# Value products with the probabilities as the stationary operand: blocks of 128 queries, normalised by query and transposed back

## The chip, the core and the metric

The kernel runs on one core of a Trainium2 chip. The metric is the device time of one execution in microseconds (us). A time given for a kernel is the median of several executions; a profile is one further execution, taken by the hardware profiler, and its times are of that execution alone. Engines are named as in the profile: PE is TensorE's stream of matmuls, PEld its loading of stationary operands (each matmul has one load ahead of it, which may run beside the matmul before), DVE is VectorE, ACT is ScalarE, POOL is GpSimd and SP is SyncE, which issues most DMAs.

## The reference

Two layers of a diffusion backbone work on 1024 latent tokens and 256 context tokens of width 1024, in float32. Layer 0 (even) holds two attentions: A, in which every query sees all 1280 keys, and B, in which a block of 128 queries sees the context and a band of three blocks, with a learned sink per head in the softmax's denominator. Each has 8 heads of 64 in 2 key/value groups. Layer 1 (odd) holds a Conformer convolution and a neighbourhood attention D with 8 heads on a 16 x 64 grid. What the change touches is the second half of every attention, the product with the values and the division by the denominator, and the gate behind it:

```python
def gqa_attend(q, k, v, bias=None, sink=None):
    s = jnp.einsum("bqhgd,bkhd->bhgqk", q, k, preferred_element_type=jnp.float32) * ATTN_SCALE
    if bias is not None:
        s = s + bias
    if sink is not None:
        sink_col = jnp.broadcast_to(sink.astype(jnp.float32)[None, :, :, None, None], s.shape[:-1] + (1,))
        p = jax.nn.softmax(jnp.concatenate([s, sink_col], axis=-1), axis=-1)[..., :-1]
    else:
        p = jax.nn.softmax(s, axis=-1)
    return jnp.einsum("bhgqk,bkhd->bqhgd", p.astype(v.dtype), v)
...
y_lat = jnp.concatenate([oa * jax.nn.silu(ag), ob * jax.nn.silu(bg)], axis=-1) @ w_out
```

## The kernel before

**Precision.** Every wide matmul is done in float32r, with operands split into a high and a low part (`hi` the rounded value, `lo` the rest): three products make one (`mm3`, lines 320 to 322). For the value product the parts are `ph` and `pl` of the probabilities and two halves of the value tile: `V[:, 0:64]` is the low part, `V[:, 64:128]` the high part, and `V[:, 128:192]` is ones, which give the denominator in 64 equal rows.

**Groups and tiles of attention.** A group is 512 columns of queries for one key/value head: 4 heads x 128 queries in layer 0, 512 queries of one head in layer 1. A tile is one block of 128 keys against these columns. Layer 0 has 40 groups (`group0`, four pairs `u`, in the order B, B, A, A, ten query blocks each) with 252 tiles, all 512 columns wide. Layer 1 has 16 groups (`group1`) of seven tiles each: two context tiles of 512 columns and five neighbourhood tiles of 384, 384, 256, 256 and 128.

**One tile** (`attn_gen`): PE computes the scores `st` (lines 477 and 481), ACT takes the exponential into `pf` (line 489) and casts it to `ph` (line 298), POOL, at times DVE, subtracts to get `pl` (line 301). Three tiles later, in `flush`, PE adds the tile's value product to `ov`, a bank of PSUM with 64 rows of output and 64 of denominator by 512 queries. It is three matmuls that stream the probabilities past a block of values: 128 columns of weights with `ph` (line 419), 64 columns with `ph` (line 420), 128 columns with `pl` (line 421). In groups B one more matmul adds the sink's share (line 424).

**The end of a group**: DVE transposes the denominator rows in 32 x 32 blocks (line 429), takes the reciprocal (431), transposes back (432), multiplies output by reciprocal (643 or 1375) and then by the gate (645 or 1377). The next group's first value product waits until the one `ov` bank has been read.

**Maxima.** A group's `prep` computes each row's maximum ahead of time (`mx` matmuls, lines 588, 600, 608, 1348, 1356, with DVE reductions), and transposes the negated maximum on PE (`trn`, line 389) into rows of the second score operand.

**What runs beside.** The attention generator (`main`) is woven with a second stream (`fill`): in layer 0 the projections of the next pair (`pq`, `pg`) and, for the last pair, the output product `po`; in layer 1 the projections `p` of D and the output product `po`. PSUM has eight banks: two `pp` (projections), two `mx`, two `st`, one `ov`, one `tr`. Where no attention runs (`solo`), projections rotate over the `pp` and the `mx` banks. `weave` gives the ratio of steps, and a scheduler then puts each engine's instructions in an order by priorities and by when it reckons that operands and banks are free. Each engine runs its list strictly in order.

Of the kernel before, what the change touches and what calls it, by code (L numbers as in the profile page):

```python
# [67 lines left out]
LATE = 100  # L68
EARLY = {2: lambda g, h, c: next(g[0].prep), 4: lambda g, h, c: h(0), 8: lambda g, h, c: c(),
# [20 lines left out]
def tile_kernel(ctx: ExitStack, tc: tile.TileContext, a, out):  # L90
# [8 lines left out]
    BUFS = {"pp": 2, "mx": 2, "st": 2, "ov": 1, "tr": 1}  # L99
# [51 lines left out]
    def mw_tile():  # L151
# [4 lines left out]
        if t == "x":  # L156
            w = mwp[0].tile([P, 1024], F32, tag="mwx", name=nm("mw"), bufs=ring.count("x"))
        else:
            w = a0.tile([P, 1920 if t == "V" else NTOK], F32, tag={"A": "KA", "B": "KB", "V": "V"}[t], name=nm("mw"),
                        bufs=2)  # L160
# [185 lines left out]
    bd = const("k_bd", [12, 4], SC, kvp)  # L346
    Ks, Vs = [], []

    def v_tiles(pool, n, bufs=1):
        Vs[:] = [pool.tile([P, n, 192], F32R, tag="V", name=nm("Vt"), bufs=bufs) for _ in range(bufs)]  # L350
        for V in Vs:
            GP.memset(V[:, :, 128:192].bitcast(F32), 1.0)
# [13 lines left out]
    def attn_prep(pool, g):  # L366
# [10 lines left out]
        nr = 12 if g.sink is not None else 4  # L377
        nmt = pool.tile([P, 12], F32R, tag="nmt", name=nm("nmt"), bufs=2)
        VE.tensor_reduce(nmt[:, 0:4], mp[:, :, 0 : g.nmp + (g.sink is not None)], axis=AX.X, op=ALU.max, negate=True)
        if g.sink is not None:  # L380
            se = pool.tile([P, 4], F32, tag="se", name=nm("se"), bufs=2)
            VE.scalar_tensor_tensor(se, nmt[:, 0:4].bitcast(F32), SCALE, sk1, op0=ALU.mult, op1=ALU.add)
# [6 lines left out]
        PE.transpose(tr2[0:nr, 0:P], nmt[:, 0:nr].bitcast(F32), ident)  # L389
        VE.tensor_tensor(QL[64 : 64 + nr, :].rearrange("p (h q) -> p h q", h=4),  # L390
                         tr2[0:nr, None, 0:P].broadcast_to([nr, 4, P]),
                         bd[0:nr, :, None].broadcast_to([nr, 4, P]), op=ALU.mult)

    def cut(ap, q, n):
        if isinstance(q, tuple):
            return ap.rearrange("p (r c) -> p r c", c=32)[:, :, q[0] : q[0] + q[1]]
        return ap[:, q : q + n]

    def flat(ap, q, n):
        return ap[:, :n].rearrange("p (r c) -> p r c", c=q[1]) if isinstance(q, tuple) else ap[:, :n]  # L400

    def attn_gen(pool, groups, vshare, look, nexts=None):
# [4 lines left out]
        cnt = [0]  # L407

        def flush():
            g, t, ph, pl = pend.pop(0)  # L410
            k, q0, n, _ = g.tiles[t]
            if t == 0:
                g.ov = bank("ov", nm("ov"))
# [4 lines left out]
            o, ph, pl = cut(g.ov, q0, n), flat(ph, q0, n), flat(pl, q0, n)  # L418
            PE.matmul(o, V[:, 64:192], ph, start=(t == 0), stop=False)  # L419
            PE.matmul(cut(g.ov[0:64], q0, n), V[:, 0:64], ph, start=False, stop=False)  # L420
            pvs.append(PE.matmul(o, V[:, 64:192], pl, start=False, stop=(last and g.sink is None)))  # L421
            if last:
                if g.sink is not None:
                    PE.matmul(g.ov, g.skm(), g.QL[0:76, :], start=False, stop=True)
                r1 = pool.tile([P, 8, 32], F32, tag="r1", name=nm("r1"), bufs=1)
                r8 = pool.tile([P, 8], F32, tag="r8", name=nm("r8"), bufs=2)
                rb = pool.tile([P, 256], F32, tag="rb", name=nm("rb"), bufs=1)
                for e in range(2):
                    VE.transpose(r1[e * 64 : (e + 1) * 64].rearrange("p a b -> p (a b)")
                                 .rearrange("p (a q) -> p a q", a=2), g.den(g.ov[64:128, :], e))  # L430
                VE.reciprocal(r8, r1[:, :, 0])
                VE.transpose(rb, r8[:, :, None].broadcast_to([P, 8, 32]))
                g.finish(g.ov, rb)
# [27 lines left out]
        for x, (g, t) in enumerate(items):  # L461
# [35 lines left out]
            prepare(x, rate // 2)  # L497
            yield
            if len(pend) > look:
                flush()  # L500
            prepare(x, rate - rate // 2)
            yield
        while pend:
            flush()
            yield
# [43 lines left out]
    def kv_tiles(u):  # L549

        if not both:
            for _ in range(2):
                both.append((a0.tile([P, NTOK], F32R, tag="KB", name=nm("KBt"), bufs=2),
                             a0.tile([P, 10, 192], F32R, tag="V", name=nm("Vt"), bufs=2)))
                GP.memset(both[-1][0][64:68, :].bitcast(F32), 1.0)
                GP.memset(both[-1][1][:, :, 128:192].bitcast(F32), 1.0)
# [12 lines left out]
    def group0(u, qb):  # L569
# [66 lines left out]
        def den(dn, e):  # L636
            return dn.rearrange("p (e f q) -> p f e q", f=2, e=2)[:, :, e, :]

        def finish(ov, rb):
            y = a0.tile([P, 2, P], F32, tag="y", name=nm("y"), bufs=YB)  # L640
            for e in range(2):
                es = slice(e * 64, (e + 1) * 64)
                VE.tensor_tensor(y[es], den(ov[0:64, :], e), rb[es, :].rearrange("p (a q) -> p a q", a=2),  # L643
                                 op=ALU.mult)
            VE.scalar_tensor_tensor(y, y, 0.5, g.gt, op0=ALU.mult, op1=ALU.mult)
# [1020 lines left out]
```

## Time and profile before

| what | value |
|---|---|
| time, median of 3 runs (range) | 1538.54 us (1535.62 to 1538.85) |
| profiled execution: its own time | 1537.48 us |
| profiled execution: span, first to last instruction | 1535.7 us |
| instructions | 21991, of these 6984 matmuls |
| mean granted TensorE clock | 0.972 |
| HBM read, written | 152.17 MB, 60.03 MB |

The stages, by the span's own clock: from 0 to 165 us the modulation vectors, norms and first projections of layer 0; from 165 to about 911 us the attention of layer 0 with its fill; then, to 1185 us, the end of layer 0 and the convolution and first D projections of layer 1; to 1500 us the attention of layer 1 with its fill; then the last output products and the final norm. Busy time per engine counts an instruction from its start to its end; matmuls overlap, so that the distance from one start to the next, here called a slot, says more about the cost of one than its duration.

### The profile page before, as it was taken

To read this page: it belongs to the slowest core of one execution; us is meant where nothing else is said; L and a number is where in the kernel's file an instruction comes from. 1 tells how busy PE (TensorE), PEld (TensorE's weight loads), DVE (VectorE), ACT (ScalarE), POOL (GpSimd) and SP (SyncE) were. 2 spreads that over 40 slices of the span, in tenths; PEclk is the share of its full clock that TensorE was granted. 3 is DMA by queue.
4 is the path that set the end of the run, shared out by engine and by line. 5 is a ranking of instruction groups with operands and counts; after the bars stand their busy time and mean duration, and the time that the engine had idled before them with its cause. 6 is when DMAs were issued, how large, how long until landed. Compare 5 with 4: busy or idle time off the path is not lost. (4 is left out here: it accounts for less than half of the span.)

```text
span 1535.7 us, 21991 instructions
## 1 busy us (share of the span) xinstructions
PE 1437.1 (94%) x6984; PEld 1165.5 (76%) x6984; DVE 1115.5 (73%) x2172; ACT 753.6 (49%) x1545; POOL 821.0 (53%) x762
## 2 busy tenths in 40 slices
PE   6989998998899989989999979999999999999995
PEld 1878977896789667768887758888877788887784
DVE  4899898589957766655467766899946775677766
ACT  2731255445444656665544665543334454555572
POOL 1462365355645767676554665865544334354665
PEclk9899999999999999999999989999999999999997
DMA  9547335522541123561111203221486667787623
GB/s 338 202 150 251 95 97 170 158 84 84 159 154 59 44 78 102 179 201 51 45 55 42 73 9 102 84 80 66 134 278 223 203 188 214 239 277 218 191 80 110
DMA packets 181163, 213.66 MB, mean 139 GB/s; under 512 B 17068, under 2 KB 134520, under 8 KB 181048
## 3 DMA queue, kind: packets, MB, share of 16 engines
q1 hardware_dynamic: 174384, 200.69, 41.8%
q10 hardware_dynamic: 6664, 11.57, 2.4%
q8 instruction: 55, 0.90, 0.2%
q14 instruction: 60, 0.49, 0.1%
HBM read 152.17 MB, written 60.03 MB: 138 GB/s over the span
## 5 line engine op out<-in xcount | busy, mean ns | idle before, releaser
L301 POOL TENSOR_TENSOR pl<-pf,ph 128x512 fp32r<-128x512 f32 (+3 forms) x321 | 392.1, 1233 | 262.9 <-ACT ph L298 215.0
L301 POOL TENSOR_TENSOR wl<-wr,wh 128x256 fp32r<-128x256 f32 (+2 forms) x256 | 193.1, 770 | 215.1 <-ACT wh L298 162.1
L489 ACT ACTIVATE pf<-st 128x512 f32<-128x512 f32 x284 | 166.1, 596 | 157.8 <-PE st L481 109.7
L298 ACT CAST ph<-pf 128x512 fp32r<-128x512 f32 (+3 forms) x364 | 205.8, 579 | 24.4 <-PE ov L420 15.9
L298 ACT CAST wh<-wr 128x256 fp32r<-128x256 f32 (+2 forms) x264 | 103.6, 404 | 162.0 <-DMA wr<-in_ev_qkv_dram 43.7
L322 PE MATMUL p<-hh,wl 128*128 128x512 f32 x448 | 175.8, 401 | 2.3 <-POOL wl L301 2.2
L320 PE MATMUL p<-hh,wh 128*128 128x512 f32 x448 | 176.7, 398 | 0.1
L321 PE MATMUL p<-hl,wh 128*128 128x512 f32 x448 | 176.6, 396 | 0.2 <-POOL hl L301 0.2
L477 PE MATMUL st<-QH,KAt 128*128 128x512 f32 (+3 forms) x364 | 141.0, 389 | 16.8 <-ACT pf L489 16.3
L419 PE MATMUL ov<-ph,Vt 128*128 128x512 f32 (+3 forms) x364 | 140.2, 385 | 8.5 <-DVE y L643 6.4
L421 PE MATMUL ov<-pl,Vt 128*128 128x512 f32 (+3 forms) x364 | 139.9, 386 | 4.4 <-POOL pl L301 3.6
L420 PE MATMUL ov<-ph,Vt 128*64 128x512 f32 (+3 forms) x364 | 137.5, 378 | 0.0
L481 PE MATMUL st<-QL,KBt 68*128 68x512 f32 (+3 forms) x364 | 136.1, 382 | 0.8 <-DVE QL L390 0.8
L1128 DVE SCALAR_TENSOR_TENSOR cps<-U,taps,cps 128x512 f32<-128x512 f32 x184 | 124.3, 748 | 0.0
L601 DVE TENSOR_REDUCE mp<-mx 128x1 f32<-128x512 f32 x128 | 85.6, 683 | 35.8 <-PE mx L600 35.0
L221 DVE SCALAR_TENSOR_TENSOR macc<-mw,csil,macc 128x512 f32<-128x512 f32 x107 | 100.8, 963 | 13.5 <-DMA mw<-in_mod_w_dram 12.7
L322 PEld LDWEIGHTS p<-hh,wl 128*128 128x128 f32 x448 | 84.4, 188 | 22.6 <-POOL wl L301 2.9
L321 PEld LDWEIGHTS p<-hl,wh 128*128 128x128 f32 x448 | 84.6, 189 | 20.1 <-POOL hl L301 0.6
L320 PEld LDWEIGHTS p<-hh,wh 128*128 128x128 f32 x448 | 84.6, 189 | 19.8 <-issue 0.6
L477 PEld LDWEIGHTS st<-QH,KAt 128*128 128x128 f32 x364 | 69.0, 190 | 37.5 <-ACT pf L489 25.4
L421 PEld LDWEIGHTS ov<-pl,Vt 128*128 128x128 f32 x364 | 69.9, 192 | 28.8 <-POOL pl L301 9.4
L419 PEld LDWEIGHTS ov<-ph,Vt 128*128 128x128 f32 x364 | 70.1, 193 | 24.8 <-issue 7.6
(277 smaller groups left out, 3507.9 us busy)
## 6 DMA issues: line engine op xcount, KB each, us to landing
mw<-in_mod_w_dram SPq DMA_DIRECT2D x34, 512.0 KB, 5.9
Q<-qs SPq DMA_DIRECT2D x40, 256.0 KB, 2.6
QH<-Q SPq DMA_DIRECT2D x80, 128.0 KB, 2.8
bm<-in_d_bm_dram SPq DMA_DIRECT2D x16, 540.0 KB, 5.8
wr<-in_od_d_dram SPq DMA_DIRECT2D x64, 128.0 KB, 2.8
mw<-in_mod_w_dram SPq DMA_DIRECT2D x28, 256.0 KB, 3.1
wr<-in_ev_qkv_dram SPq DMA_DIRECT2D x32, 192.0 KB, 3.4
KAt<-KD SPq DMA_DIRECT2D x16, 384.0 KB, 6.8
```

Source lines behind the costliest of these rows:

```text
L298: SC.copy(hi, src)
L301: (GP if leng == "g" else VE).tensor_tensor(lo, src, hi.bitcast(F32), op=ALU.subtract)
L320: PE.matmul(o, lh, rh, start=first, stop=False)
L321: PE.matmul(o, lh, rl, start=False, stop=False)
L322: done[0] = PE.matmul(o, ll, rh, start=False, stop=last)
L419: PE.matmul(o, V[:, 64:192], ph, start=(t == 0), stop=False)
L420: PE.matmul(cut(g.ov[0:64], q0, n), V[:, 0:64], ph, start=False, stop=False)
L421: pvs.append(PE.matmul(o, V[:, 64:192], pl, start=False, stop=(last and g.sink is None)))
L477: sts.append(PE.matmul(sf, KA[:, cs], cut(g.QH, q0, n), start=True, stop=False))
L481: PE.matmul(sf, KB[0:68, cs], cut(g.QL[0:68], q0, n), start=False, stop=True)
L489: SC.activation(pf[:, :n], st[:, :n], AF.Exp, scale=1.0 if g.bias else SCALE)
L1128: VE.scalar_tensor_tensor(pc, uc, w, pc, op0=ALU.mult, op1=ALU.add)
```

## The change

The value product is turned round. A block of 128 probabilities by 128 queries is the stationary operand, and the value tile, now 130 columns wide (64 low, 64 high, 2 columns of the value 2.0 in place of 64 ones), streams past it. A tile of 512 queries takes eight matmuls: per block of 128 queries one with `ph` over 130 columns and one with `pl` over the last 66. The output then stands with queries on the partitions, two blocks side by side in one bank, so a group uses two `ov` banks; to make room `pp` goes from two banks to one, and the solo rotation from four banks to three. The sink matmul goes, with the rows and constants that fed it; the sink's exponential is added by DVE.

At the group's end a new generator `norm` adds the two halves (DVE reduction over two columns per output), divides by the denominator per query, and, three steps of the attention generator later (`YD`), has PE transpose the result in two 128 x 128 blocks (`try`) into the `tr` bank, from where DVE multiplies by the gate. In layer 1 the queries of a group are laid out by blocks of 8 columns of the grid, so that each tile's queries are whole blocks of 128; the bias table and the access patterns follow.

```diff
-    BUFS = {"pp": 2, "mx": 2, "st": 2, "ov": 1, "tr": 1}
+    BUFS = {"pp": 1, "mx": 2, "st": 2, "ov": 2, "tr": 1}
...
-            tag = ("pp", "mx")[turn[0] // 2 % 2]
+            tag = ("pp", "mx", "mx")[turn[0] % 3]
...
-        Vs[:] = [pool.tile([P, n, 192], F32R, tag="V", name=nm("Vt"), bufs=bufs) for _ in range(bufs)]
+        Vs[:] = [pool.tile([P, n, VW], F32R, tag="V", name=nm("Vt"), bufs=bufs) for _ in range(bufs)]
...
-            SC.activation(nmt[:, 4:8], se, AF.Exp)
-            SC.activation(se, se, AF.Exp)
-            VE.tensor_tensor(nmt[:, 8:12], se, nmt[:, 4:8].bitcast(F32), op=ALU.subtract)
+            SC.activation(g.se, g.se, AF.Exp)
...
+        def norm(g):
+            tq = pool.tile([P, 4, 64], F32, tag="tq", name=nm("tq"), bufs=1)
+            rq = pool.tile([P, 4], F32, tag="rq", name=nm("rq"), bufs=1)
+            for e, ov in enumerate(g.ov):
+                o = ov[:, 0 : 2 * VW].rearrange("p (b x) -> p b x", b=2)
+                d = rq[:, 2 * e : 2 * e + 2]
+                VE.tensor_reduce(g.by_head(tq, e), o[:, :, 0:128].rearrange("p b (s d) -> p b d s", s=2), axis=AX.X, op=ALU.add)
+                if g.sink is not None:
+                    VE.scalar_tensor_tensor(d, g.se[:, 2 * e : 2 * e + 2], 2.0, o[:, :, 128], op0=ALU.mult, op1=ALU.add)
+                else:
+                    VE.reciprocal(d, o[:, :, 128])
+            if g.sink is not None:
+                VE.reciprocal(rq, rq)
+            tv = tq.rearrange("p (f e) d -> p f e d", e=2)
+            VE.tensor_tensor(tv, tv, g.spread(rq), op=ALU.mult)
+            for _ in range(YD):
+                yield
+            tr = bank("tr", nm("try"))
+            for k in range(2):
+                PE.transpose(tr[:, k * P : (k + 1) * P], tq[:, 2 * k : 2 * k + 2].rearrange("p a d -> p (a d)"), ident)
+            g.finish(tr[:, 0 : 2 * P].rearrange("p (k q) -> p k q", k=2))
...
-            PE.matmul(o, V[:, 64:192], ph, start=(t == 0), stop=False)
-            PE.matmul(cut(g.ov[0:64], q0, n), V[:, 0:64], ph, start=False, stop=False)
-            pvs.append(PE.matmul(o, V[:, 64:192], pl, start=False, stop=(last and g.sink is None)))
+            for j in range(n // P):
+                b = q0 // P + j
+                o = g.ov[b // 2][:, b % 2 * VW : (b % 2 + 1) * VW]
+                js = slice(j * P, (j + 1) * P)
+                PE.matmul(o, ph[:, js], V[:, 0:VW], start=(t == 0 and b % 2 == 0), stop=False)
+                pvs.append(PE.matmul(o[:, 64:VW], pl[:, js], V[:, 64:VW], start=False, stop=last and b % 2 == 1))
             if last:
-                if g.sink is not None:
-                    PE.matmul(g.ov, g.skm(), g.QL[0:76, :], start=False, stop=True)
...
-                for e in range(2):
-                    VE.transpose(r1[e * 64 : (e + 1) * 64].rearrange("p a b -> p (a b)")
-                                 .rearrange("p (a q) -> p a q", a=2), g.den(g.ov[64:128, :], e))
-                VE.reciprocal(r8, r1[:, :, 0])
-                VE.transpose(rb, r8[:, :, None].broadcast_to([P, 8, 32]))
-                g.finish(g.ov, rb)
+                ends_.append(norm(g))
+                next(ends_[-1])
...
-            VE.scalar_tensor_tensor(y, y, 0.5, g.gt, op0=ALU.mult, op1=ALU.mult)
+            VE.tensor_tensor(y, tr, g.gt, op=ALU.mult)
```

Three places in PE's list show what the scheduler makes of it. In the rows below the output's name is followed by the streaming and the stationary operand, names carry buffer numbers, the size at a row's end is the output's, and `xN` counts equal rows. The first place is the value product itself, near the end of layer 0's attention. Before, two tiles' products into the bank `ov_9297`:

```order
L419 MATMUL ov_9297<-ph_9222,Vt_1259 128x512
L420 MATMUL ov_9297<-ph_9222,Vt_1259 64x512
L421 MATMUL ov_9297<-pl_9223,Vt_1259 128x512
L419 MATMUL ov_9297<-ph_9253,Vt_1259 128x512
L420 MATMUL ov_9297<-ph_9253,Vt_1259 64x512
L421 MATMUL ov_9297<-pl_9254,Vt_1259 128x512
```

Now, seven of the eight matmuls of one tile (`ph_10766`, `pl_10767`) into the group's two banks, and the first matmul of a piece of the output product `po`:

```order
L444 MATMUL ov_10821<-Vt_1256,ph_10766 128x130
L444 MATMUL ov_10822<-Vt_1256,ph_10766 128x130
L445 MATMUL ov_10821<-Vt_1256,pl_10767 128x66
L444 MATMUL ov_10821<-Vt_1256,ph_10766 128x130
L445 MATMUL ov_10821<-Vt_1256,pl_10767 128x66
L445 MATMUL ov_10822<-Vt_1256,pl_10767 128x66
L444 MATMUL ov_10822<-Vt_1256,ph_10766 128x130
L322 MATMUL po_10129<-hc_8184,wh_10119 128x256
```

Three matmuls of 512 columns have become eight of 130 or 66, and they need not stand together: the eighth follows behind the six of this piece of `po`. The second place is the very last group of layer 0's attention. Before, PE's list holds no `po` in the last 80 rows ahead of its end, only the attention (`ov`, `st`) and a few small matmuls:

```order
L421 MATMUL ov_9583<-pl_9613,Vt_1259 128x512
L419 MATMUL ov_9583<-ph_9637,Vt_1259 128x512
L420 MATMUL ov_9583<-ph_9637,Vt_1259 64x512
L421 MATMUL ov_9583<-pl_9638,Vt_1259 128x512
L477 MATMUL st_9670<-QH_8863,KAt_5707 128x512
L481 MATMUL st_9670<-QL_8864,KBt_1258 128x512
L419 MATMUL ov_9583<-ph_9649,Vt_1259 128x512
L420 MATMUL ov_9583<-ph_9649,Vt_1259 64x512
```

Now, two tiles ahead of the end, as behind every second or third tile in this group, there stand six matmuls of `po`:

```order
L444 MATMUL ov_10822<-Vt_1256,ph_10915 128x130
L445 MATMUL ov_10822<-Vt_1256,pl_10916 128x66
L322 MATMUL po_10196<-hh_8235,wh_10119 128x512
L323 MATMUL po_10196<-hl_8236,wh_10119 128x512
L324 MATMUL po_10196<-hh_8235,wl_10120 128x512
L322 MATMUL po_10196<-hh_8235,wh_10125 128x512
L323 MATMUL po_10196<-hl_8236,wh_10125 128x512
L324 MATMUL po_10196<-hh_8235,wl_10126 128x512
L444 MATMUL ov_10821<-Vt_1256,ph_10932 128x130
L444 MATMUL ov_10822<-Vt_1256,ph_10932 128x130
L445 MATMUL ov_10821<-Vt_1256,pl_10933 128x66
```

Pieces of `po`, which need nothing of the group that is running, stand between its tiles to the end. The third place is the passage from one gate projection (`pg`) to the next, in layer 0. Before, with two `pp` banks, one follows the other directly:

```order
L320 MATMUL pg_4829<-hh_171,wh_4440 128x512
L321 MATMUL pg_4829<-hl_172,wh_4440 128x512
L322 MATMUL pg_4829<-hh_171,wl_4441 128x512
L320 MATMUL pg_4913<-hh_171,wh_4398 128x512
L321 MATMUL pg_4913<-hl_172,wh_4398 128x512
```

Now, with one bank, matmuls of the attention stand between the last of one and the first of the next:

```order
L324 MATMUL pg_5013<-hh_169,wl_4768 128x512
L500 MATMUL st_4776<-QL_4422,KBt_1255 128x512
L500 MATMUL st_4817<-QL_4422,KBt_1255 128x512
L871 MATMUL trk_4704<-ident,pc_4383 128x128 x3
L496 MATMUL st_4876<-QH_4421,KAt_1953 128x512
L499 MATMUL st_4876<-bmt,ident 128x512
L500 MATMUL st_4876<-QL_4422,KBt_1255 128x512
L322 MATMUL pg_5107<-hh_169,wh_4725 128x512
```

A projection can no longer run ahead of the one before it while that one is being read out, and the fill is spread more evenly through the attention.

More of the change, by code (lines that the diff above doesn't have):

```diff
@@ L412, in flush @@
             if t == 0:
-                g.ov = bank("ov", nm("ov"))
+                g.ov = [bank("ov", nm("ov")) for _ in range(2)]
                 if g.load_v is not None:
@@ L504, in attn_gen @@
             flush()
+            step()
+            yield
+        while ends_:
+            step()
             yield
@@ L634, in group0, with by_head, spread, finish @@
                 kt += [(k, none) for k in range(2, 10)]
-        def den(dn, e):
-            return dn.rearrange("p (e f q) -> p f e q", f=2, e=2)[:, :, e, :]
-        def finish(ov, rb):
-            y = a0.tile([P, 2, P], F32, tag="y", name=nm("y"), bufs=YB)
[L641 to L645, printed above, removed]
+        def by_head(tq, e):
+            return tq.rearrange("p (f e) d -> p e f d", e=2)[:, e]
+        def spread(rq):
+            return rq.rearrange("p (e f) -> p f e", e=2)[:, :, :, None].broadcast_to([P, 2, 2, 64])
+        def finish(tr):
+            y = a0.tile([P, 2, P], F32, tag="y", name=nm("y"), bufs=YB)
+            VE.tensor_tensor(y, tr, g.gt, op=ALU.mult)
             fs, ts = slice(2 * u, 2 * u + 2), slice(qb * P, (qb + 1) * P)
@@ L655, in group0 @@
         g = Group(load_q=load_q, start=lambda: None, last=last, bias=False, ahead=lambda t: None, rate=3 if isb else 2, gate=gate, v=lambda k: V0s[u][:, k, :], load_v=None, maxes=maxes, nmp=1 if qb < 2 else (2 if isb else 3),
-                  sink=(sink[:, hs : hs + 4], sink8[:, hs : hs + 4]) if isb else None, skm=lambda: sk, k=lambda: (KAs[u], KBs[u]),
-                  tiles=[(k, 0, 512, x) for k, x in kt], den=den, finish=finish)
+                  sink=(sink[:, hs : hs + 4], sink8[:, hs : hs + 4]) if isb else None, k=lambda: (KAs[u], KBs[u]),
+                  tiles=[(k, 0, 512, x) for k, x in kt], by_head=by_head, spread=spread, finish=finish)
         g.prep = attn_prep(kvp, g)
@@ L1381, in finish @@
                 SY.dma_start(O1d[ds, i, hf], y[ds])
-            g = Group(load_q=load_q, maxes=maxes, nmp=2, bias=True, rate=3, ahead=ahead, sink=None, tiles=tiles, den=den, finish=finish,
+            g = Group(load_q=load_q, maxes=maxes, nmp=2, bias=True, rate=3, ahead=ahead, sink=None, tiles=tiles, by_head=by_head, spread=spread, finish=finish,
                       start=start, gate=gate, last=last, load_bs=load_bs,
```

79 lines of the change are left out of this document (39 added, 40 removed).

## The prediction

> **What bounds the kernel now.** I read the page's busy shares first, then the windows of the stages, then windows of 40 us inside layer 0's attention. In a row of windows stand the stretch, its length, and for each engine its busy time with the number of instructions.
>
> ```profile
> PE 1437.1 (94%) x6984; PEld 1165.5 (76%) x6984; DVE 1115.5 (73%) x2172; ACT 753.6 (49%) x1545; POOL 821.0 (53%) x762
> ...
> 165.00:905.00 740.00, 699.99 (x3405) 566.20 (x3404) 527.15 (x1036) 388.79 (x772) 436.57 (x355) 0.98 0.32 98
> 1185.00:1500.00 315.00, 307.80 (x1565) 254.20 (x1563) 214.45 (x513) 170.71 (x379) 150.82 (x175) 0.99 0.67 199
> 200.00:240.00 40.00, 35.93 (x158) 27.64 (x159) 37.09 (x82) 22.55 (x56) 25.46 (x22) 0.88 0.45 133
> 360.00:400.00 40.00, 36.31 (x181) 28.17 (x180) 36.66 (x82) 23.28 (x57) 24.19 (x21) 1.00 0.42 127
> 520.00:600.00 80.00, 71.81 (x342) 55.44 (x342) 53.92 (x105) 49.16 (x93) 53.02 (x45) 0.96 0.28 85
> 640.00:680.00 40.00, 33.38 (x147) 23.41 (x145) 24.35 (x46) 25.80 (x45) 28.88 (x24) 1.00 0.76 239
> 680.00:880.00 200.00, 199.87 (x949) 160.54 (x947) 129.53 (x230) 103.59 (x197) 114.97 (x99) 1.00 0.18 55
> 880.00:920.00 40.00, 29.72 (x133) 21.93 (x133) 26.66 (x47) 24.79 (x49) 24.66 (x22) 0.83 0.02 7
> ```
>
> PE is the bound: 94% of the span, 699.99 of 740 us in layer 0's attention, 307.80 of 315 us in layer 1's. From 680 to 880 us it is never idle, and there every nanosecond added to PE is paid. But five windows, 240 us in all, are not full: PE is idle for 4.1, 3.7, 8.2, 6.6 and 10.3 us in them, 32.9 us. Idle that is shorter than the modelled end of a matmul doesn't show, so I also count: the full stretch does 949 matmuls in 199.87 us, 0.211 us each, and at that rate the five hold 33.3, 38.1, 72.0, 31.0 and 28.0 us of work, which leaves 6.7, 1.9, 8.0, 9.0 and 12.0 us, 37.6 together.
>
> **The price of a matmul** is its slot, from its start to the next one's. Timeline rows give start, duration, then the instruction.
>
> ```profile
> 897.28 0.39 PE L477 MATMUL st<-QH,KAt 128*128 128x512 f32 x1
> 897.51 0.39 PE L481 MATMUL st<-QL,KBt 68*128 68x512 f32 x1
> 897.75 1.05 PE L263 MATMUL bc<-ident,nr 128*128 128x128 f32 x8
> 898.55 0.47 PE L421 MATMUL ov<-pl,Vt 128*128 128x512 f32 x1
> 898.87 0.39 PE L419 MATMUL ov<-ph,Vt 128*128 128x512 f32 x1
> ...
> 902.57 0.40 PE L420 MATMUL ov<-ph,Vt 128*64 128x512 f32 x1
> ...
> 898.53 0.19 PEld L421 LDWEIGHTS ov<-pl,Vt 128*128 128x128 f32 x1
> 898.64 0.19 PEld L419 LDWEIGHTS ov<-ph,Vt 128*128 128x128 f32 x1
> ...
> 1268.60 0.22 PE L419 MATMUL ov<-ph,Vt 128*128 128x128 f32 x1
> 1268.66 0.22 PE L420 MATMUL ov<-ph,Vt 128*64 128x128 f32 x1
> 1268.72 0.28 PE L421 MATMUL ov<-pl,Vt 128*128 128x128 f32 x1
> 1268.83 0.33 PE L419 MATMUL ov<-ph,Vt 128*128 128x256 f32 x1
> ```
>
> From 898.87 to 902.57 us lie 17 matmuls of 512 columns, 16 slots: 0.231 us each. The eight of 128 columns that begin at 897.75 end where the L421 behind them really streams, one slot ahead of 898.87, at 898.64: 0.89 us for eight, 0.111 each. A stream of 128 columns alone is shorter: the L419 and L420 of layer 1's narrowest tile stand 0.06 apart. What makes 0.111 of it is the next load of 128 columns, which starts only 0.11 us behind the one before (898.53, 898.64). So a narrow matmul with 128-column weights behind it costs 0.111 us whatever it streams, and placing wide matmuls between them doesn't help, for one load is hidden behind one matmul. Between 0.060 and 0.231 I interpolate: 0.117 us for 256 columns, 0.174 for 384.
>
> **The change part by part.** The value products, with the counts of the four forms of tile, the sink's matmul, and the groups:
>
> ```profile
> L419 PE MATMUL ov<-ph,Vt 128*128 128x512 f32 x284 | 116.2, 409 | 8.5 <-DVE y L643 6.4 <-ACT ph L298 1.8 <-DMA xs<-X 0.2
> L419 PE MATMUL ov<-ph,Vt 128*128 128x384 f32 x32 | 10.8, 337 | 0.0
> L419 PE MATMUL ov<-ph,Vt 128*128 128x256 f32 x32 | 9.5, 296 | 0.0
> L419 PE MATMUL ov<-ph,Vt 128*128 128x128 f32 x16 | 3.7, 234 | 0.0
> ...
> L424 PE MATMUL ov<-QL,sk 76*128 76x512 f32 x20 | 7.9, 397 | 0.0
> ...
> L429 DVE STREAM_TRANSPOSE r<-ov 64x256 f32<-64x256 f32 x112 | 50.7, 452 | 18.1 <-PE ov L421 14.6 <-PE ov L424 1.5
> L643 DVE TENSOR_TENSOR y<-ov,rb 64x256 f32<-64x256 f32 x80 | 33.1, 413 | 0.9
> L432 DVE STREAM_TRANSPOSE rb<-r 128x256 f32<-128x256 f32 x56 | 24.6, 440 | 0.7
> L645 DVE SCALAR_TENSOR_TENSOR y<-y,gt 128x256 f32<-128x256 f32 x40 | 22.7, 568 | 0.6
> L431 DVE RECIPROCAL r<-r 128x8 f32<-128x8 f32 x56 | 11.1, 198 | 0.6
> L590 DVE TENSOR_REDUCE mp<-mx 128x2 f32<-128x512 f32 x80 | 53.5, 686 | 24.6 <-PE mx L588 24.2
> ```
>
> - Value products removed: three slots per tile, 284 x 3 x 0.231 + 32 x 3 x 0.174 + 32 x 3 x 0.117 + 16 x 0.23 (the narrowest, 1268.60 to 1268.83) = 196.8 + 16.7 + 11.2 + 3.7 = 228.4 us.
> - Added: 284 x 8 + 32 x 6 + 32 x 4 + 16 x 2 = 2624 matmuls at 0.111 = 291.3 us. The columns streamed per full tile halve (784 for 1536), yet the tile rises from 0.693 to 0.888 us, since eight loads replace three. **+62.9 us.**
> - The output's transposes: two per group, 56 groups, 112 x 0.111 = **+12.4 us**. The sink's 20 matmuls go: 20 x 0.231 = **-4.6 us**. PE's sum is **+70.7 us**: layer 0 has 252 of the full tiles (252 x 0.195 = 49.1) and 80 of the transposes (8.9), 53.4 us with the sink; layer 1 17.3 us.
>
> The trace tests the Trainium skill's page "TensorE: Matmul & The Clock Gate", section "Back-to-back issue gap", which gives about 81 ns per matmul for a sustained stream of load and matmul pairs of 128 columns. By that the 2624 would cost 212.5 us and the whole PE sum would be -12 us instead of +70.7; no run of 128-column loads in this trace goes below 0.11, so the sum goes by the rows.
>
> - The end of a group on DVE: before 2 x 452 + 198 + 440 + 2 x 413 + 568 ns = 2.94 us in layer 0. Now two reductions of 256 elements (bounds 413 from the half-height product and 686 from the reduction of 512; I take 420), two or three small operations of about 0.2, and two passes over 256 elements (0.42 to 0.57): 2.1 to 2.9 us. Where DVE isn't the bound this is worth nothing; for the wait on the one `ov` bank see the next point.
> - What the new order gives back. The windows 520 to 600, 640 to 680 and 880 to 920 are stretches of attention with little or no fill: before, `fill` ran ahead in blocks and left tiles that wait for ACT and POOL. With one `pp` bank it can't, and the order shows `po` between the tiles up to the last group. Of 29.0 us idle by count there I take back 26. In 200 to 240 and 360 to 400 DVE is busy for 37.09 and 36.66 of 40 us; fill is there already, and a lighter group end helps a little: 5 of 8.6. The rest of 165 to 905 has 40.0 - 22.6 = 17.4 us idle, from which a longer stream on PE covers 6, and of layer 1's 7.2 it covers 5. Together **-42 us**; the bounds are 0 and all of 37.6 + 17.4 + 7.2 = 62 us.
> - One `pp` bank. Each projection must now be read out before the next begins:
>
> ```profile
> L1018 DVE SCALAR_TENSOR_TENSOR x<-po,modT,x 128x512 f32<-128x512 f32 x48 | 35.8, 746 | 31.6 <-PE po L322 31.2
> ...
> L814 ACT COPY pc<-pq 128x384 f32<-128x384 f32 x40 | 18.4, 483 | 45.9 <-PE pq L322 45.9
> L341 ACT ACTIVATE sg<-pg 128x512 f32<-128x512 f32 x16 | 9.5, 595 | 24.0 <-PE pg L322 23.9
> ```
>
> A read takes 0.48 to 0.75 us, for `pg` an ACT and a DVE pass in turn, about 1.3. In the new order mostly 1.5 to 3.5 us of attention stand between two projections (between the two `pg` of the third place shown, five slots of 0.231 and three of 0.111: 1.5 us), which covers it; a few have only three transposes, 0.33. Where a projection waits, all later matmuls in PE's list wait behind it, scores too, and ACT's exponentials behind those. Some 150 projections, from none uncovered to 0.1 us each: 0 to 15, I take **+3 us**.
>
> Loads, DMAs and ACT lose only trifles (20 exponentials, one constant). The sum is 70.7 - 42 + 3 = +32 us on the profiled execution's 1537.48 us (span 1535.7 us and 1.8 us around it), which lies 1.06 us below the median of the runs: **1569 us**.
>
> **The rivals.**
> - Nothing comes back: the idle is ACT's and POOL's and moves with the tiles. For it: DVE, ACT and POOL have no window at 100%, so the waits are of order, and order may be bad again elsewhere. Against it: the stretch 680 to 880 shows that even fill leaves PE no idle. 1537.5 + 70.7 = 1608 us; from half of the gain on 1590.
> - Everything comes back: all 62 us. 1537.5 + 70.7 - 62 = 1546 us, and with DVE relieved down to no change. For it: no other engine is near its limit after 400 us.
> - The load of a probability block doesn't set the slot, so that a narrow matmul costs between its stream's 0.060 and 0.111, in the middle 0.085 us, at all 2624 + 112 places: 232.6 - 228.4 - 4.6 = -0.4, less 39 comes to 1498 us, **faster**. It decides from 0.099 us per slot downward, where 2736 slots equal 233 + 39 us. Against it: eight loads in a row at 0.111. The skill's 81 ns, named above, would give 1487 us.
> - The one `pp` bank stalls PE more often than the order reckons: 0.3 us at 150 projections is +45 in place of +3, 1611 us.
>
> **How the numbers follow.** The forecast (1552 to 1590) 0.60; nothing or little comes back 0.16 (1590 to 1608); all comes back 0.12 (1536 to 1552, a third of it within 0.2%); the bank stalls 0.06 (above 1605); cheap loads 0.06. The range from 1543 to 1608 leaves out the last, half of the last but one and part of the third, under 0.2. A measurement of this kernel tells about 0.2%, 3 us, from no change. Faster: 0.07, with a little of the third case; same: 0.05; slower: 0.88.
>
> **What would show it.** The value products' slots at 0.111 us each and about 291 us in all; PEld's busy time up by much more than PE's; PE idle in layer 0's attention well under 40 us, with the wait before the last group's first value product (6.4 us on L643 in the row of L419) gone; layer 1's attention longer by about 12 us; waits of `pq`, `pg`, `po` on their readers near nothing. Slots near 0.08, or idle that stays at 40 us, would make the prediction wrong in opposite directions.

## The result, and the profile after

| kernel | median (range) | ratio to before, 95% interval |
|---|---|---|
| before | 1538.69 us (1535.62 to 1542.42) | 1 |
| changed | 1691.05 us (1678.32 to 1702.54) | 1.0987 [1.0899, 1.1075] |

The forecast was 1569 us with a range from 1543 to 1608. The direction was right; of the rise, +152 us, it foresaw a fifth. The profiled execution took 1686.4 us (span 1684.6 us, mean granted clock 0.947, before 0.972).

The page's busy line and its groups of the value products, after:

```profile
PE 1546.2 (92%) x8608; PEld 1331.0 (79%) x8608; DVE 1060.6 (63%) x2131; ACT 756.3 (45%) x1525; POOL 818.7 (49%) x762
...
L444 PE MATMUL ov<-Vt,ph 128*128 128x130 f32 x1312 | 310.4, 294 | 4.6 <-ACT ph L300 2.8
...
L445 PE MATMUL ov<-Vt,pl 128*128 128x66 f32 x1312 | 282.0, 247 | 0.7 <-POOL pl L303 0.7
```

PE is busy for 109 us more, but its share of the span has fallen from 94% to 92%: it also waits more. Their slots, in PE's timeline (start, duration, instruction), where nothing interrupts them:

```profile
242.41 0.31 PE L444 MATMUL ov<-Vt,ph 128*128 128x130 f32 x1
242.55 0.24 PE L445 MATMUL ov<-Vt,pl 128*128 128x66 f32 x1
242.63 0.31 PE L444 MATMUL ov<-Vt,ph 128*128 128x130 f32 x1
242.78 0.24 PE L445 MATMUL ov<-Vt,pl 128*128 128x66 f32 x1
242.85 0.31 PE L444 MATMUL ov<-Vt,ph 128*128 128x130 f32 x1
```

Two pairs lie between 242.41 and 242.85: 0.22 us each, 0.11 per matmul, as predicted. So the slots aren't what was missed. Where the time went shows in windows cut at the first and last value product of each layer (stretch, length, then busy time and count of PE, PEld, DVE, ACT, POOL, granted clock, DMA share, GB/s). Before:

```profile
0.00:187.60 187.60, 162.96 (x813) 131.55 (x814) 147.46 (x244) 63.55 (x136) 67.19 (x63) 0.93 0.64 210
187.60:910.80 723.20, 679.89 (x3281) 545.30 (x3280) 515.13 (x1005) 387.09 (x765) 432.49 (x350) 0.98 0.32 98
910.80:1212.20 301.40, 294.71 (x1355) 239.06 (x1353) 231.53 (x394) 130.45 (x257) 156.88 (x165) 0.99 0.41 135
1212.20:1499.90 287.70, 281.65 (x1449) 234.11 (x1449) 196.07 (x470) 162.46 (x363) 146.97 (x169) 0.99 0.69 203
1499.90:1535.70 35.80, 17.93 (x94) 15.48 (x92) 25.27 (x60) 10.08 (x26) 17.49 (x17) 0.69 0.33 117
```

After:

```profile
0.00:180.80 180.80, 144.77 (x691) 113.81 (x692) 137.30 (x238) 62.51 (x132) 63.08 (x60) 0.90 0.65 215
180.80:939.90 759.10, 736.93 (x4589) 667.93 (x4588) 453.13 (x927) 374.55 (x725) 422.94 (x343) 0.96 0.30 90
939.90:1304.70 364.80, 327.69 (x1467) 259.92 (x1467) 260.37 (x435) 146.31 (x283) 169.73 (x176) 0.97 0.38 121
1304.70:1605.00 300.30, 286.26 (x1650) 249.88 (x1649) 174.95 (x458) 146.05 (x328) 129.55 (x147) 0.94 0.63 187
1605.00:1684.60 79.60, 50.55 (x220) 39.42 (x219) 34.86 (x75) 26.91 (x58) 33.44 (x36) 0.82 0.23 78
```

The two attentions, which the change is about, grew by 35.9 and 12.6 us. The middle between them grew by 63.4 and the tail behind the last by 43.8, though neither holds a value product. They hold 112 and 126 more matmuls than before. PE's waits (line that waits, its releaser: us, times, longest) name them, after:

```profile
PE po L322 <- DVE x L1039: 17.8, 20, 3.1
PE po L322 <- DVE x L1486: 12.0, 13, 1.8
```

And before, where L1462 is the line that is L1486 now:

```profile
PE po L320 <- DVE x L1462: 2.3, 3, 1.0
```

The output products `po` that ran as fill within the attention have been pushed out behind it, and there they run alone. In the tail's timeline:

```profile
1617.17 0.40 PE L323 MATMUL po<-od,wh 128*128 128x512 f32 x1
1617.40 0.39 PE L324 MATMUL po<-od,wl 128*128 128x512 f32 x1
1618.63 0.50 PE L322 MATMUL po<-od,wh 128*128 128x512 f32 x1 [0.84 <-DVE x L1486]
...
1621.30 0.40 PE L324 MATMUL po<-od,wl 128*128 128x512 f32 x1
1622.63 0.48 PE L322 MATMUL po<-od,wh 128*128 128x512 f32 x1 [0.94 <-DVE x L1486]
```

Twelve matmuls, then PE waits until DVE has read the one `pp` bank: 1617.40 to 1618.63 is 1.23 us from start to start where a slot is 0.23, so each group of about 4.0 us loses some 1.0 (1.1 in the next).

**An account of the span.** For each matmul record I reckon its slot at full clock: its stream (0.4545 ns per column, from the 0.233 us that lie between most matmuls of 512 columns in these traces; twice that for the modulation's `pm`), or 0.111 us if that is longer and the next load has 128 columns. What a slot takes beyond that where the granted clock is 0.5 is the half-clock extra, waits that the trace shows left out; the rest of the span is idle.

| us | span | slots at full clock | half-clock extra | idle |
|---|---|---|---|---|
| before | 1535.7 | 1370.2 | 30.8 | 134.8 |
| changed | 1684.6 | 1437.8 | 71.4 | 175.4 |
| difference | +148.9 | +67.6 | +40.6 | +40.6 |

By stage, start, layer 0's attention, middle, layer 1's attention, tail, idle changed by +13.2, -28.5, +37.3, +5.8 and +13.0 us. The clock's record lists 13 stretches at 0.5, together 89.3 us, before, and 21, together 180.3 us, after; the mean clocks agree (2 x 0.053 x 1684.6 = 179 us). The slots don't depend on how this is counted, but the split between the other two columns does: with every wait at half clock put to the clock, the differences are +51 and +31 in place of +40.6 and +40.6.

### The profile page after: what moved, and what is told of

Same layout as the page of the kernel before. It is cut to its first block, busy times and chain, and to the rows that moved or that the text cites. A ratio compares the mean times of both kernels' runs of the same rounds, so it can differ in the third digit from the quotient of the medians.

```text
span 1684.6 us, 25190 instructions
## 1 busy us (share of the span) xinstructions
PE 1546.2 (92%) x8608; PEld 1331.0 (79%) x8608; DVE 1060.6 (63%) x2131; ACT 756.3 (45%) x1525; POOL 818.7 (49%) x762
## 4 chain that ended last, share of the span: by engine, by line
PE 61%; DMA 8%; DVE 8%; issue 2%; ACT 2%; POOL 1%; SPq 1%; ACTq 0%; DVEq 0%; POOLq 0%
PE ov L444 7%; PE p L322 5%; PE p L323 5%; PE p L324 5%; PE ov L445 5%; PE po L322 5%; PE st L496 4%; PE po L323 4%; PE po L324 4%; PE st L500 3%; DMA wr<-in_od_d_dram 2%; PE mx L625 2%; DMA KAt<-KD 2%; PE pg L322 2%; PE pg L324 2%
## 5 line engine op out<-in xcount | busy, mean ns | idle before, releaser
L444 PE MATMUL ov<-Vt,ph 128*128 128x130 f32 x1312 | 310.4, 294 | 4.6 <-ACT ph L300 2.8
L445 PE MATMUL ov<-Vt,pl 128*128 128x66 f32 x1312 | 282.0, 247 | 0.7 <-POOL pl L303 0.7
L444 PEld LDWEIGHTS ov<-Vt,ph 128*128 128x128 f32 x1312 | 247.1, 195 | 17.8 <-ACT ph L300 3.2
L445 PEld LDWEIGHTS ov<-Vt,pl 128*128 128x128 f32 x1312 | 245.3, 196 | 10.3 <-POOL pl L303 1.8
L322 PE MATMUL p<-hh,wh 128*128 128x512 f32 x448 | 182.0, 408 | 3.9 <-ACT wh L300 1.8
L323 PE MATMUL p<-hl,wh 128*128 128x512 f32 x448 | 181.0, 404 | 0.6 <-DVE hl L314 0.6
L496 PE MATMUL st<-QH,KAt 128*128 128x512 f32 (+3 forms) x364 | 152.4, 420 | 1.3 <-ACT pf L508 1.2
L1039 DVE SCALAR_TENSOR_TENSOR x<-po,modT,x 128x512 f32<-128x512 f32 (+1 forms) x72 | 47.3, 659 | 99.8 <-PE po L324 94.7
L223 DVE SCALAR_TENSOR_TENSOR macc<-mw,csil,macc 128x512 f32<-128x512 f32 x107 | 89.1, 867 | 18.0 <-DMA mw<-in_mod_w_dram 17.5
L324 PE MATMUL pq<-wh,hl 128*128 128x384 f32 x256 | 91.8, 359 | 6.3 <-DVE hl L314 5.4
```

The costliest lines, as they stand in the source:

```text
L223: VE.scalar_tensor_tensor(t, w, csil[:, dk, q : q + 1], t, op0=ALU.mult, op1=ALU.add)
L322: PE.matmul(o, lh, rh, start=first, stop=False)
L323: PE.matmul(o, lh, rl, start=False, stop=False)
L324: done[0] = PE.matmul(o, ll, rh, start=False, stop=last)
L444: PE.matmul(o, ph[:, js], V[:, 0:VW], start=(t == 0 and b % 2 == 0), stop=False)
L445: pvs.append(PE.matmul(o[:, 64:VW], pl[:, js], V[:, 64:VW], start=False, stop=last and b % 2 == 1))
```

## The experiments

Each run's ratio is to the kernel before on the same chip, whose medians lay between 1536.09 and 1538.94 us. The columns behind the ratio are differences from before by the account above, in us; the last two are good to a few us, in e12 to some 15.

| run | median us | ratio [95%] | slots | half clock | idle |
|---|---|---|---|---|---|
| e1 before, one `pp` bank | 1655.01 | 1.0788 [1.0747, 1.0829] | 0 | +28 | +89 |
| e2 before, `pl` product split | 1591.26 | 1.0361 [1.0336, 1.0386] | +68 | +7 | -22 |
| e3 changed, two `pp`, `tr` in `mx` | 1646.50 | 1.0742 [1.0674, 1.0810] | +68 | +58 | -22 |
| e4 changed, two `pp`, `tr` in `pp` | 1681.74 | 1.0952 [1.0919, 1.0985] | +68 | +64 | +13 |
| e5 as e3, 192 columns | 1631.63 | 1.0601 [1.0555, 1.0648] | +68 | +24 | -6 |
| e6 as e3, 240 columns | 1626.18 | 1.0564 [1.0545, 1.0582] | +68 | +27 | -3 |
| e7 changed, 192 columns | 1672.30 | 1.0869 [1.0833, 1.0905] | +68 | +23 | +46 |
| e8 before, `tr` in `mx`, two `ov` | 1581.73 | 1.0277 [1.0250, 1.0304] | 0 | +21 | +28 |
| e9 changed, late `po` in three banks | 1672.28 | 1.0876 [1.0837, 1.0915] | +68 | +46 | +19 |
| e10 as e9, 240 columns | 1656.72 | 1.0777 [1.0750, 1.0803] | +69 | +24 | +25 |
| e11 changed, again | 1686.74 | 1.0997 [1.0955, 1.1039] | +68 | +32 | +40 |
| e12 changed, two `pp`, one `mx` | 1825.21 | 1.1835 [1.1782, 1.1889] | +69 | +247 | -5 |
| e13 as e12, 240 columns | 1680.86 | 1.0939 [1.0905, 1.0972] | +69 | +39 | +41 |

### The bank alone, and the slots alone

e1 puts the change's banks for projections into the kernel before:

```diff
-    BUFS = {"pp": 2, "mx": 2, "st": 2, "ov": 1, "tr": 1}
+    BUFS = {"pp": 1, "mx": 2, "st": 2, "ov": 1, "tr": 1}
...
-            tag = ("pp", "mx")[turn[0] // 2 % 2]
+            tag = ("pp", "mx", "mx")[turn[0] % 3]
```

> The kernel before with one `pp` bank in place of two (and the changed kernel's rotation of banks where no attention runs); value products as before. Theory BANK (the one bank pushes `po` matmuls out of the attention, where each group waits for its reader): 1600 to 1650 us, with `po` waiting on `x` for 20 us or more in all. Theory LOAD (the extra narrow matmuls and their weight loads make all of the rise, the bank nothing): 1535 to 1560 us.

e2 leaves the banks and gives PE nearly the change's added slots:

```diff
-            pvs.append(PE.matmul(o, V[:, 64:192], pl, start=False, stop=(last and g.sink is None)))
+            for j in range(n // P):
+                if isinstance(q0, tuple):
+                    oj, pj = o[:, :, 8 * j : 8 * j + 8], pl[:, :, 8 * j : 8 * j + 8]
+                else:
+                    oj, pj = o[:, j * P : (j + 1) * P], pl[:, j * P : (j + 1) * P]
+                pvs.append(PE.matmul(oj, V[:, 64:192], pj, start=False, stop=(last and g.sink is None and j == n // P - 1)))
```

> The kernel before with the product of `pl` cut into pieces of 128 columns: 284 x (4 x 0.111 - 0.231) + 32 x (3 x 0.111 - 0.174) + 32 x (2 x 0.111 - 0.117) = 69 us more of PE slots, nearly what the change adds (70.7), with the banks as before. Theory LOAD: 1670 to 1700 us, as the changed kernel. Theory BANK: 1565 to 1610 us, the slots less what idle time takes up, and `po` waits on `x` as few as before (3).

e1 came to 1655 us, above theory BANK's upper end; LOAD is out. PE's waits and the windows of the middle and the tail in e1:

```profile
PE po L320 <- DVE x L1018: 16.7, 18, 3.4
PE po L320 <- DVE x L1462: 15.2, 16, 2.7
```

```profile
912.50:1268.00 355.50, 321.23 (x1443) 255.53 (x1442) 257.83 (x430) 145.76 (x280) 167.75 (x175) 0.98 0.38 124
...
1566.60:1652.30 85.70, 55.59 (x226) 42.70 (x224) 38.45 (x77) 26.48 (x58) 34.33 (x38) 0.80 0.22 77
```

The matmuls are those of the kernel before, in another order, and yet the middle is 54 and the tail 50 us longer, with the same waits and nearly the same counts as in the changed kernel. The lost bank makes these two stages.

e2 came to 1591 us, within BANK's range: 68 us of slots lengthen the span by 53.8 us, because 22 us of idle go. In layer 0's attention idle falls from 61.4 to 31.5 us, though the fill stays much nearer to its old places than in the changed kernel. So the longer slots cover idle time by themselves; an even fill isn't needed for it.

### The bank given back

e3 has two `pp` banks in the changed kernel, with the small transposes in `mx`; e4 has them in `pp`:

```diff
-    BUFS = {"pp": 1, "mx": 2, "st": 2, "ov": 2, "tr": 1}
+    BUFS = {"pp": 2, "mx": 2, "st": 2, "ov": 2}
...
-            tag = ("pp", "mx", "mx")[turn[0] % 3]
+            tag = ("pp", "mx")[turn[0] // 2 % 2]
+        if tag == "tr":
+            tag = "mx"
```

> The changed kernel with two `pp` banks and the old rotation; the small transposes (`tr`) take their bank from `mx`, so that there are eight banks still. Theory BANK: 1570 to 1615 us, the middle near 310 us and the tail near 40. Theory LOAD: 1675 to 1700 us, no different from the changed kernel.

> As the one before it, but the small transposes take their bank from the two `pp` banks. Theory BANK: 1570 to 1625 us, perhaps 5 to 10 us behind the other since transposes and projections now wait for each other. Theory LOAD: 1675 to 1700 us.

e8 prices the sharing of `mx` in the kernel before, with the same edit there and a second `ov` bank:

> The kernel before with the small transposes in `mx` and the freed bank given to `ov` (two of them); products as before. If sharing `mx` is what kept the run with two `pp` banks at 1646 us: 1570 to 1600 us here. If it costs nothing and the second `ov` bank takes the wait of the next group's first value product away (6.4 us on L643): 1525 to 1540 us.

e3 hit neither range: it won back 45 us, with the middle at 320.5 and the tail at 40.7 us as BANK said, but layer 0's attention took 788.3 us, 29 more than in the changed kernel. e8 shows one reason: sharing `mx` costs 43 us by itself (less whatever its second `ov` bank gave back), as its first branch said. e4's 1682 us lies in LOAD's range, but its parts go with BANK: `po` waits for `x` for 2.2 us, and the middle (332.0 us) and the tail (48.8 us) are 33 and 31 us shorter than in the changed kernel. What they won, layer 0's attention lost: it takes 811.3 us, 52 more, with 493 `po` matmuls in place of 378 and a mean clock of 0.94 in place of 0.96. How much of that is the transposes' sharing of `pp` wasn't tested.

e9 lets only the late projections of each output use the `mx` banks:

```diff
-    def bank(tag, name):
-        if tag == "pp" and solo[0]:
+    def bank(tag, name, late=False):
+        if tag == "pp" and (solo[0] or late):
...
-            pp = bank("pp", nm("po"))
+            pp = bank("pp", nm("po"), fs == final or fs == parts[1] and e > 4)
...
-            pp = bank("pp", nm("po1"))[:, :n]
+            pp = bank("pp", nm("po1"), fs[0] == 4)[:, :n]
```

> The changed kernel, with the one `pp` bank for all but the last projections of each layer's output: those may also take the two `mx` banks (rotation `pp`, `mx`, `mx`). If the loss of the one bank lies where `po` runs after the attention and waits for its reader (middle +63 us, tail +44 us against before): 1605 to 1645 us, middle 320 to 340 us, tail 40 to 55. If it lies within the attention, or the pushed `po` costs the same with any banks: 1675 to 1700 us.

A miss: 1672 us, 14 below e11 on the same chip. The waits of `po` on `x` fell from 29.8 to 5.1 us and the tail to that of before, but the attentions grew. The windows of e9 behind its start:

```profile
181.60:961.10 779.50, 757.76 (x4661) 685.39 (x4659) 455.78 (x940) 376.38 (x729) 424.22 (x344) 0.96 0.29 88
961.10:1303.20 342.10, 309.16 (x1394) 249.27 (x1394) 250.96 (x422) 144.98 (x280) 168.10 (x175) 0.95 0.40 128
1303.20:1634.40 331.20, 316.60 (x1790) 275.31 (x1789) 186.30 (x475) 162.46 (x362) 146.27 (x167) 0.96 0.58 175
1634.40:1668.70 34.30, 16.25 (x81) 13.86 (x80) 22.82 (x58) 10.51 (x25) 15.98 (x16) 0.65 0.34 123
```

Against the changed kernel's windows, middle and tail lost 23 and 45 us and the attentions gained 20 and 31: 45 us of slots went back into stages that the longer value products had filled. Work that is pushed out isn't lost time; only the idle beside it was (22 us less here).

### The clock

In e3's layer 0 attention idle was 24 us, but the half-clock extra 50.8 (before 9.5, e2 11.3). Two windows of e3, the 3.4 us ahead of a fall of the clock and the stretch that follows:

```profile
610.70:614.10 3.40, 2.92 (x23) 2.70 (x24) 3.07 (x9) 0.89 (x2) 3.05 (x3) 1.00 0.30 82
614.10:641.40 27.30, 27.30 (x114) 25.36 (x114) 10.21 (x21) 12.84 (x26) 14.49 (x14) 0.50 0.24 72
```

PE waits for under 0.5 us in the first and for nothing in the second, and still runs at half clock for 27.3 us. The first holds two wide matmuls, the second of them at its very end, and 21 narrow ones: its slots fill 0.78 of it, its streams 0.38. That gave theory CLOCK. To test it, the streams are widened within the same slots, by one number:

```diff
-VW = 130
+VW = 240
```

The values are padded with columns of 2.0 that stream and are never read; e5 and e7 have 192, e6, e10 and e13 have 240.

> The changed kernel with two `pp` banks and `tr` in `mx`, and the values padded with ones to 192 columns, so that the two narrow products stream 192 and 128 columns in place of 130 and 66: the same matmuls, the same weight loads, an output that uses the first 130 columns alone. At 0.060 us for 128 columns the streams fill (0.090 + 0.060) / 0.222 = 0.68 of their slots in place of (0.061 + 0.031) / 0.222 = 0.41. Theory CLOCK (the granted clock falls to half after a stretch of about 3.4 us in which PE streams less than some 0.4 of the time, however full its slots are, and narrow products bring PE to that edge): half-clock time from 205 us to 90 to 140, time 1590 to 1620 us. Theory WAIT (half clock comes only from waits; how much a slot streams does not matter): 1635 to 1665 us, half-clock time as before it, about 205 us.

> As the one before it with 240 columns of values (streams of 240 and 176 columns, 0.113 and 0.083 us of 0.111 each). Theory CLOCK: as with 192 or up to 10 us better, 1580 to 1620 us. Theory WAIT: 1635 to 1670 us, a little slower from streams that are as long as their slots.

> The changed kernel as it is (one `pp` bank) with the values padded to 192 columns. Theory CLOCK: half-clock time from 180 us to 120 to 150, since the waits of `po` in the middle and the tail stay; time 1655 to 1675 us. Theory WAIT: 1678 to 1702 us.

> As the one before it with the values padded to 240 columns. Theory CLOCK: 15 to 20 us less than the one before it, 1590 to 1630 us, with some 30 us less at half clock. Theory WAIT: the same as the one before it within 5 us.

> The changed kernel itself, on this chip beside the two others: 1678 to 1702 us.

Each wide kernel beat its narrow one with intervals that don't touch: e3 to e5 and e6, e11 to e7, e9 to e10. The gains are 14 to 20 us. The first measurement of the changed kernel (1.0899 to 1.1075) does touch e7's, but the mean granted clocks don't: 0.957 to 0.962 in e7's four executions, 0.942 to 0.954 in the eight of the changed kernel. CLOCK had said more for e5 and e6 (1590 to 1620, 1580 to 1620), WAIT none; their times lie between the two. e7 lies where CLOCK put it; e10 is 16 us below e9, as CLOCK said, but misses its range in us, which took e9 for faster than it was. Half-clock time fell from 205 to 136 and 144 us, its extra by 34 and 31; idle rose by 16 and 19, which took half of that back.

e12 was meant as another way to a second `pp` bank:

```diff
-    BUFS = {"pp": 1, "mx": 2, "st": 2, "ov": 2, "tr": 1}
+    BUFS = {"pp": 2, "mx": 1, "st": 2, "ov": 2, "tr": 1}
...
-            tag = ("pp", "mx", "mx")[turn[0] % 3]
+            tag = ("pp", "mx", "pp")[turn[0] % 3]
```

> The changed kernel with two `pp` banks, the second taken from `mx` (one left) in place of sharing the transposes' bank. If the projections' bank is worth what the run with two `pp` banks and the price of sharing `mx` (42 us in the kernel before) suggest together: 1600 to 1630 us. If the scores' `mx` bank is as much needed: 1640 to 1690 us, with `mx` waiting on its readers.

> The run with two `pp` banks and one `mx` bank (1825 us, 578 us of it at half clock, one stretch of 116 us with PE busy throughout) with the values padded to 240 columns: the same matmuls and weight loads, streams of 240 and 176 columns in place of 130 and 66. Theory CLOCK (half clock stays as long as the streams do not fill most of a stretch of 3.4 us, and narrow products in slots set by weight loads never do): half-clock time 120 to 200 us, time 1600 to 1660 us. Theory WAIT (half clock comes from waits alone, here those of `mx` on its reader): 550 us or more at half clock, 1800 to 1850 us.

e12 missed both branches by 130 us and more, and by a road neither named: PE is without a matmul for 112 us, little more than before (99), but 578 us run at half clock. (The profiled execution took 1847.89 us; by the mean clocks of the other three, 0.856 to 0.863, it is 500 to 525 us there.) Its widened twin is the sharpest test. Layer 0's attention in one window of both, e12 first:

```profile
187.00:967.90 780.90, 748.90 (x3916) 667.60 (x3915) 395.65 (x832) 312.79 (x613) 358.47 (x295) 0.82 0.28 85
```

```profile
187.00:967.90 780.90, 737.98 (x4384) 649.73 (x4384) 452.75 (x938) 359.13 (x697) 402.98 (x329) 0.95 0.29 90
```

With more columns streamed and the same matmuls and loads, e13 does 468 matmuls more in the same stretch, at a clock of 0.95 for 0.82, and ends at 1681 us, 144 sooner.

One rival has to be met first. The matmuls are the same, but with other widths the scheduler puts them in another order: by line and operands, e12 and e13 agree in 5537 of PE's 8608 places (the changed kernel and e7 in 7937), and another order may wait elsewhere. So take a stretch of 96 matmuls in which both have the same order. In it lie 21 matmuls, 16 of them narrow, with a wait for `pl` of 0.71 us in e12 and 0.75 in e13, and then the 68 that follow. The first two rows are e12, the others e13:

```profile
379.30:382.70 3.40, 2.69 (x21) 2.51 (x20) 2.19 (x4) 1.78 (x4) 1.36 (x1) 1.00 0.16 43
382.70:399.20 16.50, 16.50 (x68) 15.10 (x67) 9.45 (x22) 7.17 (x16) 8.97 (x7) 0.50 0.14 40
```

```profile
376.70:380.10 3.40, 2.65 (x21) 2.41 (x20) 2.37 (x4) 1.69 (x4) 1.46 (x1) 1.00 0.17 43
380.10:390.30 10.20, 9.78 (x68) 8.59 (x67) 8.67 (x21) 5.78 (x14) 6.32 (x5) 1.00 0.23 64
```

In the same order and with nearly the same waits, the clock falls where the streams fill 0.41 of the 3.4 us, and stays at 1.00 where they fill 0.62. Over all stretches of at least 60 matmuls that stand in the same order, 4196 matmuls in all, e12 is at half clock for 147 us and e13 for 72. WAIT is out, and the order alone doesn't explain the gain, though how much of the 144 us it has is open. CLOCK's time (1600 to 1660) is missed by 21 us; idle rose too, by 46 us in the account, of which 11 lie between PE's records. Its half-clock time, 169 us, is within 120 to 200.

## Why the prediction was wrong, step by step

- **PE is the bound, and the slots** (+70.7 us): right. The account has +67.6, value products and transposes at 0.111. The Trainium skill's 81 ns for such pairs ("TensorE: Matmul & The Clock Gate", section "Back-to-back issue gap") isn't what this kernel pays; the rival of cheap loads is out. (By that figure PE's sum is -11 us, not -12.)
- **What the new order gives back** (-42 us): half right in place, wrong in cause. Layer 0's attention did lose 28.5 us of idle (29.9 in e2, where the banks are as before), so longer slots do it, and an even fill isn't needed. Layer 1's gave nothing back: +5.8. The working also counts the idle from 880 to 905 us twice, in the window that begins at 880 and in the rest of 165 to 905: 6.7 us (PE is busy for 18.32 of these 25), so 55 us could come back at most, not 62.
- **One `pp` bank** (+3 us, bounds 0 to 15): this step failed. Alone it costs 116.6 us of span in e1 (119 by the medians). I had looked only at the distance between projections that stay in the attention, and took "`po` between the tiles up to the last group" to mean that all of it fits there. With one bank less, 23 us of `po` slots move to the middle and 29 to the tail, where each group waits about 1 us for its reader: idle +37.3 and +13.0. With the start (+13.2) and layer 1 (+5.8) that is 69 us against +3. The rival "the bank stalls" (1611) had the right culprit, but 0.3 us at each of 150 places, none of them behind the attention.
- **The clock** had no term, and no reason was given for leaving it out: +40.6 us. Part comes with the bank's waits (e1: +28), part with the narrow streams: e7, the same kernel with wide ones, has 53.7 us of half-clock extra where two profiles of the changed kernel have 71.4 and 62.3.
- **The signs named beforehand**: PEld's busy time rose more than PE's (165 against 109 us), layer 1's attention grew by 12.6 us as forecast, but by luck (its slots count 7 less than before, since `po` left it; clock and idle make up for it), and the wait on L643 ahead of the group's first value product is gone. The waits of `po` were to be near nothing and are 30 us.
- The parts alone, 53.8 (e2) and 116.6 (e1), sum to 170, above the 149 of the changed kernel. In layer 0's attention e1 has 63.7 us of idle and the changed kernel 32.9, which can account for the gap; that the longer slots cover idle left by the bank is argued from these two, not tested by itself. What kernels without any bank shortage would take with narrow products stays open: all eight banks are in use, and each way tried to free one cost time elsewhere.

No run beat the kernel before; the nearest that turns the products round is e6, at 1626 us.

## What to carry to other kernels

Count the banks a change takes as you count its instructions, and look for what falls out of the covered stage, not only at what stays in it: a single bank is free between other work and costs a reader's wait per group where its work runs alone. A matmul whose slot is set by its weight load streams for only part of it, and that can cost a second time through the clock; where a narrow stream can be widened without a longer slot, try it. Moving pushed-out work back helps only if the covered stage still has idle time to give.

## What the runs showed of the hardware

The granted clock fell without PE being idle for long. All stretches at 0.5 are multiples of about 3.41 us. In the profiled executions of before and after, each of the 34 falls follows a 3.41 us stretch whose streams (columns at 0.4545 ns) fill at most 0.44 of it, though outside the opening stage slots fill up to 0.67. Ten stretches as low, beyond the first 10 us, were not followed by a fall, so this share is not the whole rule. One case after the change, in windows (clock in the third column from the end):

```profile
239.96:243.37 3.41, 2.05 (x17) 1.85 (x17) 3.31 (x9) 0.00 (x0) 2.10 (x2) 1.00 0.40 117
243.37:246.79 3.42, 3.42 (x17) 3.24 (x16) 0.07 (x1) 0.73 (x2) 1.27 (x1) 0.50 0.29 73
246.79:250.20 3.41, 3.41 (x16) 3.31 (x16) 1.37 (x3) 2.95 (x6) 1.44 (x2) 0.50 0.19 63
250.20:253.60 3.40, 3.40 (x13) 3.11 (x13) 1.23 (x2) 0.60 (x1) 1.07 (x1) 0.50 0.40 110
253.60:257.03 3.43, 3.43 (x13) 3.24 (x12) 1.66 (x5) 1.95 (x4) 2.56 (x3) 0.50 0.12 38
257.03:260.40 3.37, 3.37 (x20) 3.19 (x19) 2.73 (x8) 2.31 (x5) 2.27 (x4) 1.00 0.41 117
```

A wait of 1.4 us and seven pairs of narrow products bring the fall, and four such stretches, with PE busy throughout, pass before it ends. PE's timeline there:

```profile
243.45 0.46 PE L444 MATMUL ov<-Vt,ph 128*128 128x130 f32 x1
243.71 0.36 PE L445 MATMUL ov<-Vt,pl 128*128 128x66 f32 x1
243.88 0.46 PE L444 MATMUL ov<-Vt,ph 128*128 128x130 f32 x1
```

At half clock the ratio stays: a pair takes 0.43 us for 0.18 us of streams, so with three wide matmuls of 0.46 us a tile's four pairs stream (0.71 + 1.39) / (1.72 + 1.39) = 0.68 of their time with PE never idle. In these two executions half clock ended at shares from 0.69 up and stayed at some up to 0.86; three matmuls of 512 columns, 0.233 us apart at full clock, stream all the time. Within layer 0's attention the longest stretch at half clock is 6.8 us before, 13.7 after, 27.3 in e3 and 116.1 in e12; in e6 and e13, with wide streams, 6.8, but for one of 10.2 at e13's end of that stage.

The Trainium skill, page "TensorE: Matmul & The Clock Gate", section "What's actually happening", names a free-running window of 3413 ns, and the traces agree with its length. It puts half clock down to an idle window; here the one quoted from e3 was 86% busy (2.92 of 3.40 us) and a fall followed. e12 and e13, with the same 21 matmuls and nearly the same waits in one such stretch, show that the share streamed matters; where exactly it decides wasn't measured.
